# Hybrid decoder trunk: 43 elementwise instructions per MLP move from POOL to DVE

## The chip, the cores and the metric

The kernel runs on one core of one Trainium2 chip. The metric is the time of one execution on the device in microseconds (us), of which the median over several runs is given. The engines are called by their short names: PE is TensorE, PEld its weight loads, DVE VectorE, ACT ScalarE, POOL GpSimd, SP SyncE, whose queue (SPq) issues all of the kernel's DMAs.

## The reference, cut to what matters

The trunk takes 1024 tokens of width 1024, puts 16 meta tokens ahead of them, and runs two layers: a Mamba-2 mixer and an MLP, then a latent-attention mixer and an MLP. What the change touches is the beginning of each MLP:

```
def rms_norm(x, gain):
    y = xf * lax.rsqrt(jnp.mean(xf * xf, axis=-1, keepdims=True) + EPS)
    return (y * gain)
def sqrelu_mlp(h, w_up, w_down):
    return jnp.square(jax.nn.relu(h @ w_up)) @ w_down
...
h = h + sqrelu_mlp(rms_norm(h, ln_mlp[i]), mlp_w_up[i], mlp_w_down[i])
```

`w_up` is 1024 x 4096, `w_down` 4096 x 1024, all in float32.

## The kernel before

**Precision.** Each float32 operand is split into a hi part in the matmul's format (`fp32r`), made by an ACT cast, and a lo part, the source minus the hi part, made by a `tensor_tensor` on DVE or POOL. Each product is three matmuls: hi x hi, hi x lo, lo x hi (`mm_k`, lines 604 to 606 of the profile).

**Strassen's scheme.** Both matrix products of an MLP are done with Strassen's seven products in place of eight. Tokens are cut into two halves (520 each in MLP 0, 512 in MLP 1), the width of 1024 into two halves, and the 4096 hidden columns into 16 units of 256, each in two halves of 128. A unit has the products P1 to P7. P1 and P2 take the plain inputs; P6, P7, P5 and P4 take sums and differences of the input's quarters (`x_sums`), and of the unit's weight quarters (`block`). P3 takes another plain quarter.

**The order at the beginning.** The ones matmuls that give the normalisation are late on purpose in the program: products are made from the inputs times gain, and `hidden` multiplies by the reciprocal root mean square (`rb`) once it is known. First come P1 and P2 of eight units, 16 products (`pre`); their weights are loaded in pairs of units (`prep0`, line 794). Between them `x_sums(k)` makes the four summed inputs, a quarter of each at a time, and `rstd(0)` the normalisation of half 0, from the sum of squares that `sum_squares(0)` added up. Then P6, P7, P5 and P4 of unit 0 run together in four PSUM tiles (`first`), which are all the PSUM tiles there are in this phase. `sum_squares(1)`, the input of P3 and `rstd(1)` follow in the program, and then the items of units 0 to 15 one after another, each weight prepared three items ahead (`prep`).

**The weights' lo parts.** `w_item` (line 598 is its lo part, 596 its hi part on ACT) counts the weights (`lo_n`) and gives every odd one to POOL and every even one to DVE, unless the caller asks for DVE with `on_v`. The down projection always does.

**Buffers.** `whl` holds five split weights, `raw` two raw weight tiles of 1 MB, `pu` five partial products, `c11` two; `t1`, `t2`, `ta`, `tb` of `x_sums` have one buffer each. The loads of raw weights (lines 794 and 645) wait until the tile's last readers, the casts and lo parts, are done. All DMAs stand in SP's queue, in order.

**Order on each engine.** The program is written in the order above, and the order in which each engine runs its instructions is made when the kernel is built: a scheduler plays the program through with a cost model, takes the ready instruction that comes first in the program, and places the waits. On the chip each engine then runs its own list in that order.

**PSUM.** A product is evacuated by ACT (P1, line 714) or by DVE (`add`, line 710). `hidden` is line 681 (DVE) and 682 (ACT), with the DMA of line 684. The output projection ahead of MLP 0 and MLP 1 is evacuated by DVE into `h` (line 466).

Of the kernel before, what the change touches and what calls it, by code (L numbers as in the profile page):

```python
# [9 lines left out]
F32 = mybir.dt.float32  # L10
# [4 lines left out]
ALU = mybir.AluOpType  # L15
# [4 lines left out]
P = 128  # L20
# [26 lines left out]
def trunk(ctx: ExitStack, tc, x, meta, ln_mix, ln_mlp, w_in, conv_w, conv_b, dt_bias, a_log, d_skip,  # L47
# [3 lines left out]
    V, S, G, PE = nc.vector, nc.scalar, nc.gpsimd, nc.tensor  # L51
# [501 lines left out]
    HK = KD // 2  # L553
# [4 lines left out]
    def mlp(layer, tok, w, close_h):  # L558
# [22 lines left out]
        def raw_tile():  # L581
            return rawp.tile([P, 4 * n], F32, name="raw")
# [9 lines left out]
        def w_item(src, on_v=False):  # L592

            k, m = src.shape[1:]
            wt = whl.tile([P, 2, 512], F32R, name="whl")[:, :, :k * m].rearrange("p a (k m) -> p a k m", k=k)
            S.copy(wt[:, 0], src)  # L596
            lo_n[0] += 1
            (G if lo_n[0] % 2 and not on_v else V).tensor_tensor(wt[:, 1], src, wt[:, 0].bitcast(F32), ALU.subtract)  # L598
            return wt
# [22 lines left out]
        rb = misc.tile([P, 2, n], F32, name="rb")  # L622
# [9 lines left out]
        def pu():  # L632
            return misc.tile([P, n], F32, name="pu", bufs=5)

        class Unit:
# [33 lines left out]
            def prep(self, p):  # L669
                if p == "P6" and self.u < NPRE:  # L670
                    self.p1 = pu()
                    nc.sync.dma_start(self.p1, p1_d[self.u])
                self.W[p] = w_item(self.block(p))

            def hidden(self, half, i, name):

# [77 lines left out]

        def x_split(xt, k, src):
            S.copy(xt[:, k, 0, :], src)  # L756
            G.tensor_tensor(xt[:, k, 1, :], src, xt[:, k, 0, :].bitcast(F32), ALU.subtract)

        def sum_squares(half, new):
            for k in range(KD):  # L760
                src = h[:, k, hslice[half]]
                if k == 0:
                    S.activation(rb[:, half, :], src, AF.Square)
                else:
                    sq = new()
                    S.activation(sq, src, AF.Square)
                    G.tensor_tensor(rb[:, half, :], rb[:, half, :], sq, ALU.add)

        def rstd(half, new):

# [16 lines left out]
        units = [Unit(u) for u in range(NPRE)]  # L787
        pair = [None]

        def prep0(u, j):  # L790
            if j == 0:
                if u % 2 == 0:
                    pair[0] = raw_tile()[:, :KD * 2 * P].rearrange("p (i k m) -> p i k m", i=2, k=KD)
                nc.sync.dma_start(pair[0][:, u % 2], w_up[layer, :, u * 256:u * 256 + P].rearrange("(k p) m -> p k m", p=P))
            units[u].W["P%d" % (j + 1)] = w_item(pair[0][:, u % 2, j * HK:(j + 1) * HK, :])

        tmp_stack = ExitStack()
        tp = tmp_stack.enter_context(tc.tile_pool(reuse_waits="tile", name="utmp", bufs=1))
# [1 line left out]
        for a in pre[:4]:  # L800
            prep0(*a)
        for p, j in (("P1", 0), ("P2", 1)):
            for k in range(HK):
                x_plain(X[p], k, j, 0)
        sum_squares(0, pu)
        for half in range(2):
            nc.sync.dma_start(hsp[:, :, half, :], h[:, :, hslice[half]])

        def x_sums(k):
            g1, g2 = gcol_(k), gcol_(HK + k)  # L810
            h11, h12 = [h[:, k, s_] for s_ in hslice]
            h21, h22 = [h[:, HK + k, s_] for s_ in hslice]

            def tmp(name):
                return tp.tile([P, n], F32, name=name)

            b11, t1, t2 = tmp("ta"), tmp("t1"), tmp("t2")
            S.activation(b11, h11, AF.Copy, scale=g1)
            V.scalar_tensor_tensor(t1, h12, g1, b11, ALU.mult, ALU.subtract)
            V.scalar_tensor_tensor(t2, h22, g2, t1, ALU.mult, ALU.subtract)  # L820
            x_split(X["P6"], k, t2)
            b12 = tmp("ta")
            S.activation(b12, h12, AF.Copy, scale=g1)
            V.scalar_tensor_tensor(b12, h22, g2, b12, ALU.mult, ALU.subtract)
            x_split(X["P7"], k, b12)
            x_split(X["P5"], k, t1)
            b21 = tmp("tb")
            S.activation(b21, h21, AF.Copy, scale=g2)
            V.tensor_tensor(b21, t2, b21, ALU.subtract)
            x_split(X["P4"], k, b21)  # L830

        for i, (u, j) in enumerate(pre):
            if i + 4 < len(pre):
                prep0(*pre[i + 4])
            units[u].run("P%d" % (j + 1))
            if i == 1:
                rstd(0, pu)
            if i % 4 == 3:
                x_sums(i // 4)
# [3 lines left out]
        for k in range(HK):  # L843
            for p in ORDER[2:6]:
                mm_k(first[p], units[0].W[p], X[p], k, k == 0, k == HK - 1)
        sum_squares(1, lambda: tp.tile([P, n], F32, name="sq", bufs=2))
        tmp_stack.close()
        X["P3"] = up.enter_context(tc.tile_pool(reuse_waits="tile", name="ux3", bufs=1)).tile([P, HK, 2, n], F32R, name="xP3")
# [196 lines left out]
        for j, g in enumerate(prods):  # L1045
            f, c, p = g
# [67 lines left out]
    with ExitStack() as st:  # L1114
# [5 lines left out]
        sq = [sm.tile([P, T], F32, name=f"asq{i}") for i in range(2)]  # L1120
# [430 lines left out]
```

## Time and profile before

| | |
|---|---|
| median of 3 runs | 3000.17 us (2999.78 to 3005.01) |
| profiled execution | 3008.28 us |
| its span, first to last instruction | 3006.6 us |
| mean granted TensorE clock | 0.983 |
| PE busy | 2882.3 us, 96% of the span |
| DVE busy | 2231.1 us, 74% |
| ACT busy | 1283.4 us, 43% |
| POOL busy | 1114.1 us, 37% |

The span is one execution seen by the hardware profiler. An engine's busy time counts its instructions' own times, and waits inside an instruction once it has begun are in it. PE's matmuls are pipelined, so a listed matmul can be longer than the step to the next one. MLP 0 begins at about 960 us of the span (its first matmul at 982), MLP 1 at about 2336 us (first matmul at 2353).

### The profile page before, as it was taken

Reading aid. Unit: us, or ns where it says so; the run is one execution under the profiler, and the core shown is the slowest. Engines: PE = TensorE matmul, PEld = TensorE weight load, DVE = VectorE, ACT = ScalarE, POOL = GpSimd, SP = SyncE. Lnnn points to the kernel's source line nnn. Section 1 sums busy time; section 2 is a strip of 40 time slices with the busy share of each in tenths; the row PEclk is TensorE's granted clock in tenths of the full one; section 3 lists DMA queues with packets and bytes.
Section 4 is the critical chain, followed back from the end, with each engine's and each line's share of the span. In section 5 each row is a group of like instructions: output and inputs, shape, how many; then the busy total and the mean of one; then the engine's idle time right before and its main releaser. Section 6 shows DMA issues by size and latency. Waiting matters only on the chain. (4 is left out here: it accounts for less than half of the span.)

```text
span 3006.6 us, 48412 instructions
## 1 busy us (share of the span) xinstructions
PE 2882.3 (96%) x18221; PEld 2579.1 (86%) x18221; DVE 2231.1 (74%) x3904; ACT 1283.4 (43%) x2539; POOL 1114.1 (37%) x996
## 2 busy tenths in 40 slices
PE   7999999999899899999999889899999999999999
PEld 7999999999799899999999777677777777888887
DVE  6678877778856898875685477778774898876664
ACT  4334333334432633343443446456552643343442
POOL 2345444444764722210021454554554732210010
PEclk9999999999999999999999989899999999999999
DMA  3233333334633455479883101001132455479753
GB/s 110 63 70 78 63 73 72 73 70 105 170 111 97 163 179 198 154 264 359 306 285 106 44 23 26 20 27 33 30 120 87 155 175 203 161 280 342 265 182 104
DMA packets 326660, 409.32 MB, mean 136 GB/s; under 512 B 31341, under 2 KB 199234, under 8 KB 323354
## 3 DMA queue, kind: packets, MB, share of 16 engines
q1 hardware_dynamic: 326426, 406.24, 42.9%
q8 instruction: 143, 2.34, 0.3%
q14 instruction: 91, 0.75, 0.1%
HBM read 300.23 MB, written 105.88 MB: 135 GB/s over the span
## 5 line engine op out<-in xcount | busy, mean ns | idle before, releaser
L604 PE MATMUL mps<-hhl,whl 128*128 128x260 f32 (+1 forms) x1472 | 440.5, 300 | 8.5 <-DVE c L710 4.2
L606 PE MATMUL mps<-hhl,whl 128*128 128x260 f32 (+1 forms) x1472 | 436.6, 297 | 8.0 <-DVE whl L598 4.3
L605 PE MATMUL mps<-hhl,whl 128*128 128x260 f32 (+1 forms) x1472 | 437.7, 298 | 0.1
L98 PE MATMUL psm<-hn,whl 128*128 128x346 f32 (+4 forms) x1176 | 388.9, 331 | 6.0 <-DVE zs L269 4.4
L99 PE MATMUL psm<-hn,whl 128*128 128x346 f32 (+4 forms) x1176 | 386.5, 329 | 0.3 <-DVE hn L221 0.3
L100 PE MATMUL psm<-hn,whl 128*128 128x346 f32 (+4 forms) x1176 | 382.5, 326 | 1.1 <-POOL whl L93 1.1
L604 PEld LDWEIGHTS mps<-hhl,whl 128*128 128x128 f32 x1472 | 278.0, 189 | 19.1 <-issue 4.8
L606 PEld LDWEIGHTS mps<-hhl,whl 128*128 128x128 f32 x1472 | 279.0, 190 | 17.8 <-DVE whl L598 5.4
L605 PEld LDWEIGHTS mps<-hhl,whl 128*128 128x128 f32 x1472 | 278.2, 189 | 8.5 <-issue 0.5
L598 DVE TENSOR_TENSOR whl<-draw,whl 128x512 fp32r<-128x512 f32 x208 | 150.4, 735 | 172.5 <-ACT whl L596 172.4
L93 POOL TENSOR_TENSOR whl<-wraw,whl 128x1024 fp32r<-128x1024 f32 (+3 forms) x95 | 226.4, 2384 | 139.9 <-ACT whl L90 134.6
L596 ACT CAST whl<-draw 128x512 fp32r<-128x512 f32 x208 | 128.7, 622 | 324.8 <-PE mps L606 169.8
L604 PE MATMUL mps<-xP,whl 128*128 128x260 f32 (+1 forms) x768 | 246.5, 321 | 11.1 <-ACT xP L756 3.4
L606 PE MATMUL mps<-xP,whl 128*128 128x260 f32 (+1 forms) x768 | 245.9, 321 | 5.4 <-DVE whl L598 5.4
L605 PE MATMUL mps<-xP,whl 128*128 128x260 f32 (+1 forms) x768 | 246.1, 320 | 0.0
L98 PEld LDWEIGHTS psm<-hn,whl 128*128 128x128 f32 (+1 forms) x1176 | 220.9, 188 | 13.8 <-DVE zs L269 4.7
L100 PEld LDWEIGHTS psm<-hn,whl 128*128 128x128 f32 (+1 forms) x1176 | 220.6, 188 | 6.2 <-issue 3.3
L998 POOL TENSOR_TENSOR mP<-mP,mP 128x520 f32<-128x520 f32 (+1 forms) x28 | 43.3, 1568 | 492.5 <-DVE mP L995 432.6
L99 PEld LDWEIGHTS psm<-hn,whl 128*128 128x128 f32 (+1 forms) x1176 | 221.1, 188 | 4.8 <-issue 1.7
L598 POOL TENSOR_TENSOR whl<-raw,whl 128x512 fp32r<-128x512 f32 x64 | 95.4, 1494 | 217.8 <-ACT whl L596 96.5
L612 PE MATMUL mps<-whl,hhl 128*128 128x512 f32 x448 | 173.8, 389 | 0.3 <-DVE whl L598 0.3
L613 PE MATMUL mps<-whl,hhl 128*128 128x512 f32 x448 | 174.0, 389 | 0.0
(386 smaller groups left out, 7972.4 us busy)
## 6 DMA issues: line engine op xcount, KB each, us to landing
draw<-in_mlp_w_down_dram SPq DMA_DIRECT2D x52, 1024.0 KB
raw<-in_mlp_w_up_dram SPq DMA_DIRECT2D x32, 1024.0 KB
raw<-hid SPq DMA_DIRECT2D x28, 1040.0 KB
raw<-hid SPq DMA_DIRECT2D x28, 1024.0 KB
hid<-stg SPq DMA_DIRECT2D x96, 260.0 KB
wraw<-in_ssd_w_in_dram SPq DMA_DIRECT2D x48, 512.0 KB
hid<-stg SPq DMA_DIRECT2D x96, 256.0 KB
acsb<-acs_d SPq DMA_DIRECT2D x64, 256.0 KB
```

The lines of the kernel that those rows point to most:

```text
L93: eng_lo.tensor_tensor(lo, src, hi.bitcast(F32), ALU.subtract)
L98: PE.matmul(ps, whi, xhi, start=i == 0, stop=False)
L99: PE.matmul(ps, whi, xlo, start=False, stop=False)
L100: PE.matmul(ps, wlo, xhi, start=False, stop=i == n - 1)
L596: S.copy(wt[:, 0], src)
L598: (G if lo_n[0] % 2 and not on_v else V).tensor_tensor(wt[:, 1], src, wt[:, 0].bitcast(F32), ALU.subtract)
L604: PE.matmul(ps[:, i, :], wt[:, 0, k, :], xt[:, k, 0, xs_], start=first, stop=False)
L605: PE.matmul(ps[:, i, :], wt[:, 0, k, :], xt[:, k, 1, xs_], start=False, stop=False)
L606: PE.matmul(ps[:, i, :], wt[:, 1, k, :], xt[:, k, 0, xs_], start=False, stop=last)
L612: PE.matmul(ps[:, 0, :], xt[:, k, 0, qs], wt[:, 1, 0, :], start=False, stop=False)
L613: PE.matmul(ps[:, 0, :], xt[:, k, 1, qs], wt[:, 0, 0, :], start=False, stop=last)
L998: G.tensor_tensor(out_, out_, a, ALU.add)
```

## The change

Four edits in `mlp`, which runs twice. `x_split` and `sum_squares` call DVE (`V`) in place of POOL (`G`) for the lo part and for the addition. `prep0` asks `w_item` for DVE for all its 16 weights (P1 and P2 of eight units), and `prep` does so for units 0 and 1 (ten weights: P6, P7, P5, P4 and P3 of each). The counter `lo_n` still counts each weight, so the later weights keep their engines. Per MLP these are 2 x 7 additions, 16 lo parts of inputs and 13 lo parts of weights, since the other 13 of the 26 were on DVE before.

```
@@ -670 (Unit.prep)
-                self.W[p] = w_item(self.block(p))
+                self.W[p] = w_item(self.block(p), self.u < 2)
@@ -754 (x_split)
             S.copy(xt[:, k, 0, :], src)
-            G.tensor_tensor(xt[:, k, 1, :], src, xt[:, k, 0, :].bitcast(F32), ALU.subtract)
+            V.tensor_tensor(xt[:, k, 1, :], src, xt[:, k, 0, :].bitcast(F32), ALU.subtract)
@@ -764 (sum_squares)
                     S.activation(sq, src, AF.Square)
-                    G.tensor_tensor(rb[:, half, :], rb[:, half, :], sq, ALU.add)
+                    V.tensor_tensor(rb[:, half, :], rb[:, half, :], sq, ALU.add)
@@ -792 (prep0)
-            units[u].W["P%d" % (j + 1)] = w_item(pair[0][:, u % 2, j * HK:(j + 1) * HK, :])
+            units[u].W["P%d" % (j + 1)] = w_item(pair[0][:, u % 2, j * HK:(j + 1) * HK, :], True)
```

## Rows read from the trace of the kernel before

**Rows 1.** The page's first part: busy time, share of the span and instructions of each engine.

```profile
PE 2882.3 (96%) x18221; PEld 2579.1 (86%) x18221; DVE 2231.1 (74%) x3904; ACT 1283.4 (43%) x2539; POOL 1114.1 (37%) x996
```

**Rows 2.** The windows view of both beginnings; each engine's busy time and instruction count, granted clock.

```profile
982.00:1053.20 71.20, 60.03 (x468) 58.79 (x468) 62.27 (x59) 45.51 (x78) 54.02 (x33) 0.95 0.52 172
2353.00:2421.50 68.50, 59.22 (x232) 46.19 (x233) 60.91 (x60) 44.90 (x78) 53.19 (x33) 0.90 0.54 177
```

**Rows 3.** PE's timeline, its longest gaps: start, length, engine, line, [idle before <- releaser].

```profile
1011.58 0.39 PE L604 MATMUL mps<-hhl,whl 128*128 128x260 f32 x1 [1.94 <-DVE c L710]
...
1043.02 0.58 PE L604 MATMUL mps<-xP,whl 128*128 128x260 f32 x1 [2.89 <-ACT pu L714]
...
2391.04 0.50 PE L606 MATMUL mps<-hhl,whl 128*128 128x512 f32 x1 [2.25 <-POOL whl L598]
...
2410.88 0.80 PE L606 MATMUL mps<-xP,whl 128*128 128x512 f32 x1 [3.19 <-DVE whl L598]
```

**Rows 4.** PE's timeline where nothing holds it back: first and last of a run.

```profile
1047.68 0.28 PE L604 MATMUL mps<-xP,whl 128*128 128x260 f32 x1
...
1052.23 0.29 PE L606 MATMUL mps<-xP,whl 128*128 128x260 f32 x1
...
2418.11 0.40 PE L605 MATMUL mps<-hhl,whl 128*128 128x512 f32 x1
...
2421.97 0.39 PE L604 MATMUL mps<-xP,whl 128*128 128x512 f32 x1
```

**Rows 5.** DVE's and then POOL's timeline where both work.

```profile
1021.30 1.80 DVE L829 TENSOR_TENSOR tb<-t,tb 128x520 f32<-128x520 f32 x1
1023.03 1.77 DVE L656 TENSOR_TENSOR s<-raw 128x512 f32<-128x512 f32 x1
1024.73 0.68 DVE L710 TENSOR_TENSOR c<-pu,mps 128x520 f32<-128x520 f32 x1
...
1022.51 1.74 POOL L757 TENSOR_TENSOR hhl<-t,hhl 128x520 fp32r<-128x520 f32 x1
1024.22 1.71 POOL L598 TENSOR_TENSOR whl<-raw,whl 128x512 fp32r<-128x512 f32 x1
```

**Rows 6.** DVE's timeline where POOL is idle.

```profile
1004.23 0.75 DVE L819 SCALAR_TENSOR_TENSOR t<-h,prm,ta 128x520 f32<-128x520 f32 x1
1004.90 1.31 DVE L681 SCALAR_TENSOR_TENSOR c<-c,rb 128x520 f32<-128x520 f32 x2
...
2429.98 0.68 DVE L598 TENSOR_TENSOR whl<-s,whl 128x512 fp32r<-128x512 f32 x1
2430.58 0.68 DVE L775 TENSOR_SCALAR stg<-mps 128x512 f32<-128x512 f32 x1
```

**Rows 7.** The windows view of the sums of squares (line 767) ahead of the first beginning: POOL's busy time.

```profile
960.00:974.00 14.00, 10.98 (x7) 1.00 0.18 66
```

**Rows 8.** DVE's timeline at the end of the output projection ahead of MLP 0.

```profile
966.82 1.13 DVE L753 SCALAR_TENSOR_TENSOR hhl<-h,prm,hhl 128x520 fp32r<-128x520 f32 x1
967.87 0.75 DVE L466 TENSOR_TENSOR h<-h,psm 128x260 f32<-128x260 f32 x2
...
980.34 0.43 DVE L466 TENSOR_TENSOR h<-h,psm 128x260 f32<-128x260 f32 x1 [0.30 <-PE psm L100]
```

**Rows 9.** The waits view of the first beginning, then of the second: who waited for whom, us, times.

```profile
POOL whl L598 <- ACT whl L596: 7.2, 2, 6.9
POOL xP L757 <- ACT xP L756: 7.1, 2, 4.1
...
POOL xP L757 <- ACT xP L756: 6.1, 5, 2.6
...
POOL whl L598 <- ACT whl L596: 4.8, 3, 1.9
```

**Rows 10.** The DMA queue's (SPq) and DVE's timeline: a load and its first reader.

```profile
2385.27 0.38 SPq L645 DMA_DIRECT2D raw<-in_mlp_w_up_dram  x1
...
2392.03 1.21 DVE L656 TENSOR_TENSOR s<-raw 128x512 f32<-128x512 f32 x1 [0.49 <-DMA raw<-in_mlp_w_up_dram]
```

## The prediction

> **What bounds the kernel now.** I read the page's first part first: TensorE (PE) is busy for 96% of the span, DVE as the next engine for 74% [rows 1]. So a change on DVE and POOL can pay only where PE stands still or runs slowly, and only up to that loss. I next asked for PE's timeline around both places where the changed lines run, the beginnings of the two MLPs, and found a row of gaps there, of which the four shown last 1.9 to 3.2 us [rows 3]. Their releasers are of three kinds: a PSUM evacuation (line 710 on DVE, 714 on ACT) and a weight's lo part (line 598), on POOL or on DVE. The gap at 1043.02 stands with ACT's copy, which itself was queued behind work that waited for DVE.
>
> The windows view then sizes the loss. The first beginning is taken from the first MLP matmul to the first sum product (982 to 1053.2), the second likewise (2353 to 2421.5) [rows 2]. Where nothing holds PE back, 39 matmuls of 260 columns start in a row with 38 steps between 1047.68 and 1052.23, 0.1197 us each, and 17 steps of 512 columns take 3.86 us, 0.2271 us each [rows 4]. PE's own need is thus 468 x 0.1197 = 56.0 us of the 71.2, and 232 x 0.2271 = 52.7 us of the 68.5 [rows 2, 4]. What is lost is 15.2 and 15.8 us, 31.0 in all. Part of it is the clock: the mean granted clock is 0.95 and 0.90 in these windows [rows 2], since it falls to the lower level, 1.2 GHz, behind some of the gaps: the matmuls at 1043.02 and 2410.88 took 0.58 and 0.80 us, those behind two shorter gaps 0.39 and 0.50 [rows 3]. That loss goes if the gaps go.
>
> In both windows DVE is the fullest engine beside PE: 62.27 and 60.91 us, for only 59 and 60 instructions, more than 1 us each [rows 2]. The reason is in its timeline. Where POOL works too, a DVE instruction with two SBUF inputs takes 1.77 to 1.80 us and starts 1.7 us after the one before, POOL's own take 1.7 us and follow at that same step, and the two alternate; DVE's line 710, with one input in PSUM, takes 0.68 us in the middle of it [rows 5]. Where POOL is idle, the same kind of DVE instruction takes 0.68 us and the next starts after 0.60 us, and one with a scalar pointer after 0.67 us [rows 6]. So here a POOL instruction costs DVE about 1.1 us (1.7 less 0.60), more than the 0.60 us of doing that work itself.
>
> **The change, part by part.** *What moves.* Per MLP it is 7 adds per half of the tokens, 16 lo parts of input sums, and the half of 26 weight lo parts that POOL had: 14 + 16 + 13 = 43 instructions, of which POOL runs 33 inside each window [rows 2]. The seven adds of half 0 run ahead of it, with 10.98 us of POOL [rows 7]; the other lo parts lie at its edges.
>
> *DVE's load in the windows.* Of the 59 present instructions 16 (lines 753, 819, 820, 824, four each) are of the kind with a scalar pointer: 16 x 0.67 + 43 x 0.605 = 36.7 us without POOL beside them. The 33 added make 20.0 us. Together 56.7, against 62.27 now: DVE gains 5.6 us while it does more. In the second, 16 x 0.66 + 44 x 0.60 + 33 x 0.60 = 56.8 against 60.91: 4.1 us. (0.605 and 0.66 are the same steps at 520 and 512 columns, estimated from [rows 6].)
>
> *What the end gains.* From below: if DVE's queue sets the end and idles as long as now (8.9 and 7.6 us, window less busy time), the gain is 5.6 + 4.1 = 9.7 us. From above: if PE runs at its own pace throughout, 31.0 us. Both ends are close to one another in kind, since DVE's 56.7 us would just fit beside PE's 56.0. For the upper end speaks that some of DVE's work is not needed in time: the seven adds of half 1 (4.2 us), four of line 753 (2.7 us) and the sums of unit 1's weights feed only later products, and now they stand behind everything else. Against it speaks that two engines at full load in order never fit without gaps. I take the middle, 20.4 us.
>
> *The stretch before.* The adds of half 0 come to DVE while it evacuates the output projection (line 466). They add 7 x 0.60 = 4.2 us and take POOL's brake off line 753, which now takes a step of 1.05 us (966.82 to 967.87) in place of 0.67 [rows 8], 7 x 0.38 = 2.7 us: 1.5 us more per MLP. At most this delays PE by 3.0 us in sum, since PSUM buffers free later. At the least it costs nothing: the adds are needed only by the ones matmuls after unit 0, and later DVE idles 0.30 us before each line 466 [rows 8]. I take 1.5 us.
>
> *Queues.* POOL issues no DMA. SP's loads of later weights wait for lo parts, because those release the raw buffers; the lo parts come earlier, so the loads do too. A load of 1 MB was issued at 2385.27 and its first reader waited only 0.49 us for it at 2392.03 [rows 10], so a load takes 6.8 us and is not what holds this stage. On ACT nothing is added. Behind each moved lo part on DVE now stand the evacuations that give PE its PSUM buffer; that is the price of a misplaced one, 0.60 us plus whatever that lo part waits for on ACT.
>
> *Sum.* 20.4 less 1.5 is 18.9, say 19 us. The profiled execution took 3008.28 us (span 3006.6), 8.1 above the median of the runs; its windows go into the difference alone: 3000.2 less 19 is 2981 us.
>
> *A rule against it.* DVE is busy for 87% and 89% of the windows [rows 2], and POOL for 76% and 78%. The Trainium skill (Perfetto Trace Analysis, Optimizing Scalar/DVE Operations) says that work may be worth moving from a saturated DVE to GpSimd, which is the reverse of this change; in the same place it warns that the two share an SBUF read port, so that it might not help. By the rule without the warning this change would be slower, by the first rival's sum; the trace bears out the warning [rows 5, 6].
>
> **The rivals.** *DVE's present busy time is all its own.* Then the added work comes on top: 62.27 + 20.0 + 8.9 = 91.2 us in place of 71.2, and 20 us again in the second window, with 8.4 us of adds before them: +48, 3048 us. That is the case the skill's rule would make. Against it: the same line 598 at 0.68 us and the same line 656 at 1.77 [rows 5, 6]. Chance 0.03.
>
> *Waits for ACT move into DVE's queue* (the slower side). Each moved lo part needs ACT's cast of the same tile, just made. On POOL such waits were free: 7.2 + 7.1 us in the first window, 6.1 + 4.8 in the second, 25.2 in all [rows 9]. On DVE they stop evacuations. It decides at 9.7 us more of DVE idle, where the lower bound is used up. With all of them, 25.2 - 9.7 + 3.0 = +18.5: 3019 us. For it: ACT's casts in turn wait for DVE's sums, a round trip in the middle of every input sum. Against it: on DVE other ready instructions lie between, and POOL waited mostly because it had nothing else. Chance 0.09.
>
> *The same with about half of them*: 12.6 - 9.7 + 1.5 = +4.4, 3005 us, nothing that can be measured; or the gain is there and later stages take it back. Chance 0.14.
>
> *PE at its own pace in both windows, adds in DVE's gaps*: -31, 2969 us. Chance 0.05.
>
> **How the numbers follow.** The forecast has the other 0.69, and its own range is 2971 to 2993: the bounds 9.7 - 3.0 = 6.7 and 31.0 - 1.5 = 29.5 us below 3000.2. About 0.2% (6 us) is what a measurement of this kernel can tell from no change; the runs lie 5 us apart. Faster by more: 0.69 + 0.05 = 0.74; within: 0.14; slower: 0.03 + 0.09 = 0.12. The range reaches from 2970, almost at PE's own pace, to 3001, which takes in the nearer half of the cases without a change; left out are the slower ones (0.12), the other half (0.07) and some 0.01 below.
>
> **What would show it.** In the profile after, DVE's two-input instructions in both windows should take 0.68 to 0.76 us throughout, POOL should be nearly idle there, DVE's instruction count should rise by 33 per window while its busy time falls to about 57 us, and the first sum product should be evacuated about 10 us earlier after the first MLP matmul in each. PE's gaps of 2 to 3 us should mostly be gone and the clock at 1.00. It is wrong if DVE keeps its 1.8 us instructions with POOL idle, if DVE's waits for ACT grow past 5 us a window, or if the windows shrink and the span doesn't.

## The result and the profile after

The changed kernel takes 2973.2 us in the median of four runs (2966.9 to 2984.1), against 3002.1 for the kernel before in four (2999.8 to 3005.0). The ratio is 0.9896, with a 95% interval of 0.9875 to 0.9916: 28.9 us less. Measured a second time beside the kernel before, the changed kernel was 22.9 us faster (run e9 below). The profiled execution took 2973.4 us, its span is 2971.7.

The page's first part, which answers to [rows 1]:

```profile
PE 2871.9 (97%) x18221; PEld 2571.5 (87%) x18221; DVE 2225.1 (75%) x3990; ACT 1284.7 (43%) x2539; POOL 980.8 (33%) x910
```

POOL has 86 instructions and 133 us less, DVE 86 instructions more and 6 us less. That is the change in one line: 86 instructions were added to DVE and its busy time fell.

The windows view of the two beginnings, which answers to [rows 2]. Each window runs from the first MLP matmul to the evacuation of the first sum product; the columns are the window, its length, busy time (x instructions) of PE, PEld, DVE, ACT and POOL, the granted clock, the DMA share and GB/s:

```profile
977.20:1034.54 57.34, 57.30 (x475) 57.21 (x476) 54.85 (x90) 44.89 (x78) 0.00 (x0) 1.00 0.65 209
2332.99:2388.78 55.79, 55.31 (x242) 45.14 (x241) 54.91 (x91) 43.55 (x75) 0.00 (x0) 1.00 0.63 208
```

The same two windows in the kernel before, from its own first matmul to its own evacuation; the second began 1 us ahead of the 2353 that the prediction took:

```profile
982.35:1053.27 70.92, 60.10 (x468) 58.83 (x469) 61.92 (x58) 45.16 (x78) 54.02 (x33) 0.95 0.53 173
2351.98:2421.49 69.51, 59.89 (x235) 46.46 (x234) 61.92 (x61) 45.71 (x79) 53.31 (x33) 0.90 0.53 174
```

The first has shrunk from 70.9 to 57.3 us, the second from 69.5 to 55.8. POOL runs nothing in either. DVE runs 90 and 91 instructions in 54.9 us each, 0.609 and 0.603 us per instruction, and the granted clock is 1.00, its upper level of 2.4 GHz, in place of 0.95 and 0.90. PE's own need is now 475 x 0.1197 = 56.9 and 242 x 0.2271 = 55.0 us [rows 4]: it runs at its own pace but for 0.5 and 0.8 us. DVE is busy for 7.1 us less in the first window and 7.0 in the second than before, and idle for 6.5 and 6.7 us less.

DVE's timeline in a stretch like that of [rows 5], the same lines 829 and 656:

```profile
1012.86 0.70 DVE L829 TENSOR_TENSOR tb<-t,tb 128x520 f32<-128x520 f32 x1
1013.47 0.70 DVE L757 TENSOR_TENSOR hhl<-t,hhl 128x520 fp32r<-128x520 f32 x1
1014.08 0.69 DVE L656 TENSOR_TENSOR s<-s,raw 128x512 f32<-128x512 f32 x1
1014.68 0.70 DVE L710 TENSOR_TENSOR c<-pu,mps 128x520 f32<-128x520 f32 x1
```

Both took 1.8 us before and take 0.70 and 0.69 now, and the next one starts 0.61 and 0.60 us after them.

Not all of DVE's shorter busy time is the missing brake. Four instructions of line 753 stood inside each window before, the first of them at 1046.85 in MLP 0; in the new order they stand behind its end:

```profile
1046.85 0.75 DVE L753 SCALAR_TENSOR_TENSOR xP<-h,prm,xP 128x520 fp32r<-128x520 f32 x1
```

```profile
1034.54 0.70 DVE L710 TENSOR_TENSOR pu<-pu,mps 128x520 f32<-128x520 f32 x1 [1.43 <-PE mps L606]
1035.15 0.75 DVE L753 SCALAR_TENSOR_TENSOR xP<-h,prm,xP 128x520 fp32r<-128x520 f32 x1
```

At a step of 0.67 us they are 2.7 us per window that moved and weren't saved. Of the other side of the prediction's account, the end of the output projection [rows 8], here is DVE's timeline, and then the view of the projection's matmuls ahead of MLP 0 with their first and last start:

```profile
963.16 0.75 DVE L753 SCALAR_TENSOR_TENSOR hhl<-h,prm,hhl 128x520 fp32r<-128x520 f32 x1
963.83 0.42 DVE L466 TENSOR_TENSOR h<-h,psm 128x260 f32<-128x260 f32 x1
964.16 0.69 DVE L767 TENSOR_TENSOR rb<-rb,pu 128x520 f32<-128x520 f32 x1
964.78 0.42 DVE L466 TENSOR_TENSOR h<-h,psm 128x260 f32<-128x260 f32 x1
```

```profile
L100 PE MATMUL psm<-oact,whl x400: 277/318/511, 753.4 to 976.4; 128*128 128x348 f32 x57, 128*128 128x346 f32 x55, 128*128 128x260 f32 x22
```

The adds of line 767 now stand between the evacuations; line 753 starts 0.67 us ahead of the next instruction, not 1.05. From first to last matmul the projection takes 223.0 us, against 221.6 before (759.9 to 981.5). Of PE's gaps [rows 3] these remain, the first behind the window, the second at the very start of the other, the third in the later units, where POOL still makes half of the weights' lo parts:

```profile
1042.20 0.39 PE L604 MATMUL mps<-hhl,whl 128*128 128x260 f32 x1 [1.78 <-DVE pu L710]
...
2334.53 0.50 PE L606 MATMUL mps<-hhl,whl 128*128 128x512 f32 x1 [0.47 <-DVE whl L598]
...
2480.53 0.50 PE L606 MATMUL mps<-xP,whl 128*128 128x512 f32 x1 [1.26 <-POOL whl L598]
```

**Where the 34.9 us between the two spans went.** Shrunk windows 13.6 + 13.7 = 27.3; behind the second window 2.2; the projection ahead of MLP 0 cost 1.4. The rest, some 6.8 us, lies outside of what was changed: the Mamba mixer's first products (line 100), which the change doesn't touch, end at 743.1 us in place of 749.6. How far such stretches vary is seen in the changed kernel's second run: its windows sum up to 113.1 us again, but from the end of the first to the start of the second it took 1305.9 us, in place of 1298.5 here, and its median was 2980.5 us. Times of two kernels therefore differ by several us for reasons that don't concern the change, and where that matters the text below goes by the sum of the two windows, taken in each profile in the same way. It is 140.4 us before and 113.1 after.

### The profile page after: what moved, and what is told of

It reads as the page before. It is cut to its first block, busy times and chain, and to the rows that moved or that the text cites. A ratio compares the mean times of both kernels' runs of the same rounds, so it can differ in the third digit from the quotient of the medians.

```text
span 2971.7 us, 48357 instructions
## 1 busy us (share of the span) xinstructions
PE 2871.9 (97%) x18221; PEld 2571.5 (87%) x18221; DVE 2225.1 (75%) x3990; ACT 1284.7 (43%) x2539; POOL 980.8 (33%) x910
## 5 line engine op out<-in xcount | busy, mean ns | idle before, releaser
L598 POOL TENSOR_TENSOR whl<-s,whl 128x512 fp32r<-128x512 f32 x42 | 64.5, 1539 | 343.8 <-ACT whl L596 291.9
```

## The experiments

Two theories were set against each other. The *brake*: a POOL instruction that reads SBUF holds up DVE's two-input instructions, so that it costs DVE more than doing the work itself. The *latency*: DVE makes a lo part in 0.69 us where POOL needs 1.3 to 1.75, so what waits for it gets it sooner. A third, that the build's new order on each engine brought the gain, is tested beside them.

**The change in parts.** Three kernels move one part each, a fourth moves all lo parts and leaves all additions on POOL.

```
e1_inputs_only:     x_split alone:        G.tensor_tensor -> V.tensor_tensor
e2_weights_only:    w_item alone:         on_v=True in prep0, self.u < 2 in prep
e3_squares1_only:   sum_squares, half 1:  (V if half else G).tensor_tensor
e8_squares_on_pool: e1 and e2 together, sum_squares on G
```

> Only the 16 lo parts of input sums per MLP go to DVE. Brake theory (each POOL instruction with SBUF inputs costs DVE about 1.1 us, whatever it computes, against 0.60 us on DVE itself): 16 of the 33 instructions per window, so about half of the 26.3 us that the two windows shrank by, 10 to 15 us faster than before, some 2988 us, and two-input DVE instructions beside POOL's remaining ones still at 1.7 to 1.8 us. Latency theory (what pays is that the lo part which PE or ACT waits for is made in 0.69 us in place of 1.3 to 1.75): no PE gap of before was released by one of these lo parts, so 0 to 4 us.

> Only the 13 weight lo parts per MLP go to DVE. Brake theory: 10 of 33 per window, 6 to 10 us faster than before, some 2994 us. Latency theory: these are the lo parts that PE waited for (3.8 us of its gaps in the second window, and the weight loads behind them), so this part alone brings most of the gain, 15 us or more.

> Only the 7 additions of half 1 per MLP go to DVE; no product waits for them before the second normalisation. Brake theory: 7 of 33 per window, 4 to 8 us faster than before, some 2996 us. Latency theory: nobody waits for them, so they bring nothing or cost their 4 us of DVE per MLP: 3002 to 3008 us.

> The changed kernel with all 14 additions of squares per MLP on POOL as before: only the lo parts are on DVE. Brake theory: 7 instructions of POOL in each window cost DVE about 0.95 us each in place of 0.60, 2 to 3 us per window, and the stretch before it gains 1.4 us in MLP 0: 1 to 5 us slower than the changed kernel, 2974 to 2978 us, though the run with only these additions moved showed no gain at all. Latency theory: no product waits for them, 2970 to 2973 us.

The medians were 2983.6, 3001.9 and 3006.0 us against 3001.7 for the kernel before beside them, ratios 0.9940 (0.9918 to 0.9963), 0.9991 (0.9978 to 1.0005) and 1.0007 (0.9996 to 1.0018); the fourth 2987.3 against 3005.3, 0.9941 (0.9922 to 0.9960). The windows views in this order:

```profile
977.40:1039.43 62.03, 58.21 (x470) 56.88 (x471) 60.82 (x74) 45.96 (x79) 31.12 (x17) 1.00 0.59 191
2335.44:2398.22 62.78, 56.49 (x242) 44.51 (x241) 61.64 (x76) 45.94 (x79) 32.27 (x17) 1.00 0.56 186
```

```profile
976.50:1045.62 69.12, 60.11 (x468) 58.75 (x469) 64.30 (x69) 45.27 (x79) 37.86 (x23) 0.95 0.54 177
2337.16:2404.93 67.77, 59.00 (x235) 45.28 (x234) 64.02 (x72) 45.16 (x78) 37.49 (x23) 0.95 0.51 168
```

```profile
981.10:1053.71 72.61, 62.33 (x468) 60.11 (x469) 64.95 (x65) 45.43 (x78) 42.09 (x26) 0.95 0.53 169
2354.33:2422.37 68.04, 60.57 (x235) 46.49 (x234) 61.83 (x68) 45.47 (x78) 41.18 (x26) 0.92 0.55 178
```

```profile
976.60:1035.56 58.96, 58.57 (x482) 58.04 (x483) 58.89 (x86) 45.48 (x79) 11.07 (x7) 1.00 0.64 207
2332.26:2393.40 61.14, 59.33 (x254) 47.06 (x253) 60.53 (x88) 46.48 (x81) 11.89 (x7) 1.00 0.59 192
```

The build orders the instructions anew in each kernel, so a different number of matmuls stands ahead of a window's end. PE's own need in the table is that number times its step, 0.1197 and 0.2271 us [rows 4]; what remains of the window is lost. All are sums of both windows, in us.

| kernel | POOL instructions in each window | windows | PE's own need | lost |
|---|---|---|---|---|
| before | 33 | 140.4 | 109.4 | 31.0 |
| squares of half 1 moved (e3) | 26 | 140.7 | 109.4 | 31.3 |
| weights moved (e2) | 23 | 136.9 | 109.4 | 27.5 |
| inputs moved (e1) | 17 | 124.8 | 111.2 | 13.6 |
| inputs and weights moved (e8) | 7 | 120.1 | 115.4 | 4.7 |
| all moved, the changed kernel | 0 | 113.1 | 111.8 | 1.3 |

Moving the inputs alone saved 15.6 us of the windows, the weights alone 3.5, the squares alone nothing, the first two together 20.3. The squares brought 7.0 more once the rest was gone, but only 3.4 of them are lost time; for the others fewer matmuls stand ahead of the end, and line 753 stood inside the windows in e8 and not in the changed kernel.

The first part has the size that the brake theory expected, and is not the 0 to 4 us of the latency theory. But in that run DVE's busy time fell by only 1.1 and 0.3 us; what fell was its idle time, from 9.0 and 7.6 to 1.2 and 1.1 us. The second part fell short of what the brake theory expected, and of what the latency theory expected by far more. The third is a miss for the brake theory as it was put, a fixed price per POOL instruction, and it is what the latency theory expected. The fourth is a miss for both: 2987.3 us, where 2974 to 2978 and 2970 to 2973 were expected.

The DVE column says why a fixed price fails. With 0.609 us for each DVE instruction, as in the changed kernel, the rest of DVE's busy time in a window is what POOL costs it: in the first window 61.92 - 58 x 0.609 = 26.6 us for POOL's 33 instructions in the kernel before, 0.81 each; 25.4 for 26 in the third run, 0.98; 22.3 for 23 in the second, 0.97; 15.8 for 17 in the first, 0.93; 6.5 for 7 in the fourth, 0.93. In the second window the same sums give 0.75 in the kernel before, and 0.79, 0.88, 0.90 and 0.99. Counted in DVE's timelines, the 33 instructions stretched 28 of its two-input instructions beyond 0.9 us in either window; 26 stretched 25 and 23, 23 stretched 22 and 20, 17 stretched 17, 7 stretched 6. So POOL's many instructions in the kernel before hit fewer than one of DVE's each, and to take some away removes in part those that hit none: moving seven additions took 1.2 and 4.4 us of brake away and put 7 x 0.609 = 4.3 us of work on DVE in each window. Which ones miss, and why, no run shows. In the fourth run the time rose by more than the windows account for, 14 us against 7, as far as kernels measured at different times can be compared; its profile is that of its fastest run, 2979.0 of 2979.0 to 2994.0, so what the slower ones lost was not seen.

**POOL work that nobody waits for.** Three kernels are the changed kernel with POOL instructions added whose results are never used, at each of the 16 input sums and at each of the 7 additions of half 1, in both MLPs. The order of all instructions on PE, DVE, ACT and SP, as the traces list them, is exactly that of the changed kernel.

```
+ scr = tp.tile([P, n], F32, name="scr")
  # in x_split; likewise in sum_squares if half, where e4 adds and e11 copies its own source
e4_pool_reads:       + G.tensor_tensor(scr, h[:, k, hslice[0]], h[:, k, hslice[1]], ALU.subtract)
e11_pool_one_input:  + G.tensor_copy(scr, h[:, k, hslice[0]])
e5_pool_memsets:     + for _ in range(3): G.memset(scr, 0.0)
```

> The changed kernel with 23 more POOL instructions per MLP that nobody waits for: one subtraction of two SBUF tiles at each input sum, one addition at each square of half 1, their results never used. Brake theory: each holds up DVE by about 0.9 us, 55 + 23 x 0.9 = 76 us of DVE per window in place of 55, so windows of 70 to 76 us in place of 57 and 56, and 26 to 38 us slower than the changed kernel: 2999 to 3011 us, about the time of the kernel before. Latency theory, and the theory that the build's new order brought the gain: nothing waits for these results, so 2973 us.

> The same places as the run before, but each additional POOL instruction is three memsets of the same tile, which read nothing in SBUF. If the brake comes from what POOL reads, DVE stays at 0.69 us and the time at 2973 us. If any POOL work brakes DVE, then 1.8 us instructions on DVE again and 2990 us or more.

> The changed kernel with 23 more POOL instructions per MLP that nobody waits for, each a copy with one SBUF input. If POOL's reading from SBUF is what brakes DVE, one input is enough: DVE instructions at 1.3 to 1.8 us again, windows of 65 us or more, 2990 us or more. If it takes two inputs on both sides, 2973 us.

The medians: 3020.9 us with two inputs (ratio to the kernel before 1.0051, 1.0031 to 1.0071), 2983.5 with one (0.9941, 0.9922 to 0.9960; the changed kernel beside it 2980.5, with an interval that overlaps), 2975.1 with none (0.9899, 0.9880 to 0.9918). Two inputs: the windows view, then DVE's and POOL's timeline.

```profile
985.50:1063.04 77.54, 63.44 (x482) 62.00 (x483) 77.50 (x89) 45.23 (x77) 36.81 (x23) 0.93 0.46 152
2361.05:2438.70 77.65, 62.27 (x245) 47.58 (x244) 77.53 (x91) 45.23 (x76) 36.68 (x23) 0.92 0.44 149
```

```profile
1000.49 1.82 DVE L828 SCALAR_TENSOR_TENSOR ta<-h,prm,ta 128x520 f32<-128x520 f32 x1
1002.23 1.82 DVE L768 TENSOR_TENSOR rb<-rb,sq 128x520 f32<-128x520 f32 x1
...
994.96 10.28 POOL L758 TENSOR_TENSOR scr<-h 128x520 f32<-128x520 f32 x6
```

One input, the same views:

```profile
979.40:1041.79 62.39, 59.19 (x482) 58.32 (x483) 62.35 (x90) 44.89 (x77) 22.01 (x23) 1.00 0.57 189
2333.55:2396.44 62.89, 58.79 (x247) 46.60 (x245) 62.89 (x92) 44.84 (x76) 21.68 (x23) 0.97 0.56 184
```

```profile
994.83 1.11 DVE L757 TENSOR_TENSOR xP<-tb,xP 128x520 fp32r<-128x520 f32 x1
995.86 1.10 DVE L598 TENSOR_TENSOR whl<-raw,whl 128x512 fp32r<-128x512 f32 x1
...
978.97 16.41 POOL L758 COPY scr<-h 128x520 f32<-128x520 f32 x16 [23.14 <-PE psm L100]
```

No input:

```profile
978.90:1036.19 57.29, 57.29 (x475) 57.17 (x476) 55.09 (x89) 45.01 (x78) 36.57 (x69) 1.00 0.65 210
2333.22:2389.22 56.00, 55.52 (x243) 45.31 (x242) 55.12 (x92) 43.96 (x75) 36.16 (x69) 1.00 0.64 207
```

```profile
989.29 0.69 DVE L757 TENSOR_TENSOR xP<-tb,xP 128x520 fp32r<-128x520 f32 x1
989.90 0.69 DVE L598 TENSOR_TENSOR whl<-raw,whl 128x512 fp32r<-128x512 f32 x1
...
996.77 0.81 DVE L785 TENSOR_SCALAR pu<-pu 128x520 f32<-128x520 f32 x1
...
984.92 10.60 POOL L759 MEMSET scr<- 128x520 f32 x18
```

The first of these decides between the theories. Nothing waits for these 23 instructions and no engine's order changed, yet the windows grew from 113.1 to 155.2 us, past the 140.4 of the kernel before, and the changed kernel became slower than that; the time lies above the 2999 to 3011 us that the brake theory gave. So the new order alone doesn't make the kernel fast; that it adds nothing, as with line 753, isn't shown. DVE is busy for all of both windows; its instructions beside POOL's take 1.8 us and step at 1.74, and 77.50 - 89 x 0.609 = 23.3 us are lost on 23 instructions of POOL, 1.01 us each. A copy with one input takes POOL 0.97 us, and DVE's two-input instructions then step at 1.03: 0.33 us lost for each, windows of 125.3 us. That lies between the two outcomes that were expected, 65 us or more for each window and no effect at all, and the medians alone don't tell it from the changed kernel. Three memsets in its place kept POOL busy for 36.6 us, about the same as the 23 reading instructions, and DVE's two-input instructions stayed at 0.69: 113.3 us. So it is POOL's reading of SBUF that brakes DVE, and a stretched DVE instruction steps as POOL's own do beside it: 1.74 us against 10.28 / 6 = 1.71, and 1.03 against 16.41 / 16 = 1.03. The Trainium skill (SBUF — State Buffer, Who interferes with whom) says this of a DVE instruction with two SBUF inputs: it contends with a GpSimd instruction that reads SBUF, not with one that only writes it. The three runs agree, with 1.8, 1.1 and 0.69 us.

**Additions of half 0, and the remaining weights.**

```
e6_half0_on_pool:        after, sum_squares: (V if half else G).tensor_tensor
e7_all_weights_dve:      after, prep: w_item(self.block(p), True)
e12_all_weights_again:   the same kernel as e7
e10_weights_half0:       e7 and e6 together
e9_after_again:          the changed kernel
```

> The changed kernel, with the 7 additions of half 0 back on POOL, which run beside the end of the output projection. The prediction's term for that stretch: they cost 1.5 us per MLP at most on DVE, so 0 to 3 us faster than the changed kernel, some 2972 us, with the first MLP matmul 1.4 us sooner after the projection's first. If the price of the adds is instead hidden, no difference; if the brake on line 753 and on the first splits matters more than the adds, up to 4 us slower, 2977 us.

> The changed kernel with all weight lo parts of the up projection on DVE, those of units 2 to 15 too. Brake theory: about 56 POOL instructions per MLP cost DVE some 0.9 us each and would cost 0.60 there, so DVE's queue loses up to 17 us per MLP of work, but PE stands still there for only a few us in all: 2 to 8 us faster than the changed kernel, 2965 to 2971 us. If a full DVE sets the pace and the brake is of no account, 5 to 30 us slower, since 34 us of work per MLP come on top.

> The changed kernel once more, on the same chip as the next two, so that small differences can be read: 2970 to 2976 us by every theory.

> All weight lo parts of the up projection on DVE, once more beside the changed kernel. If the 4 us of the first comparison are real, 2 to 6 us faster than the changed kernel in this call; if not, within 2 us.

> The same with the additions of half 0 back on POOL. The projection ahead of MLP 0 took 221.6 us with them there and 223.0 with them on DVE, so 1 to 2 us faster than the run before it if the windows stay at 57 and 54 us, and the fastest of all; equal if the first window pays it back.

With half 0 on POOL the projection takes 221.6 us again (753.7 to 975.3), so the 1.4 us are those adds; the windows view:

```profile
976.20:1033.49 57.29, 57.29 (x475) 57.17 (x476) 54.72 (x90) 44.82 (x78) 0.00 (x0) 1.00 0.65 209
2329.37:2386.12 56.75, 56.74 (x247) 45.76 (x245) 55.83 (x92) 45.84 (x79) 0.00 (x0) 1.00 0.63 204
```

The windows sum up to 114.0, and the median of 2974.7 us (ratio 0.9906, 0.9889 to 0.9923) can't be told from the changed kernel's. The changed kernel run again took 2980.5 us beside 3003.4 for the kernel before (0.9924, 0.9907 to 0.9941), outside of the 2970 to 2976 that was expected by every theory. All weight lo parts on DVE gave 2969.2 us (0.9879, 0.9860 to 0.9897), and, beside that second run of the changed kernel, 2976.6 (0.9907, 0.9887 to 0.9926): 4 us faster than the changed kernel both times, though the first time they weren't measured beside one another, with intervals that overlap. With both edits it was 2968.3 us (0.9878, 0.9858 to 0.9899), 12 us below the changed kernel measured beside it and with an interval clear of its own; 1 to 2 us below the run with all weights was expected, and it is 8. Its windows don't show this (114.4 us); behind the second one its profile has 577.0 us where the changed kernel's has 583.0, and why isn't shown. It has the lowest median here; but the ratio of one and the same kernel moved by 0.003 between two measurements, and 0.9879 was reached without the additions on POOL, so how much of the 12 us it has everywhere isn't settled. The windows view of the same stretch in the later units, the changed kernel and then this one, shows what the last step does:

```profile
2400.00:2500.00 100.00, 97.69 (x428) 79.49 (x427) 97.48 (x140) 36.77 (x60) 33.76 (x18) 1.00 0.63 214
```

```profile
2400.00:2500.00 100.00, 100.00 (x442) 82.34 (x441) 96.02 (x160) 40.20 (x65) 0.00 (x0) 1.00 0.63 211
```

With POOL out of it DVE ran 20 instructions more in less busy time, and PE, which had stood still for 2.3 us, had none of it.

## Why the prediction was right

It had the direction, the mechanism and a range that holds the time; its size, 19 us against 28.9, was too small, and 2973.2 us lies near the end of its range, close to the 2969 of the rival with PE at its own pace. Point by point:

- *A POOL instruction costs DVE about 1.1 us, the work itself 0.60.* The second is 0.609. The first was too high for the kernel before: 0.81 and 0.75 on average, and 0.79 to 1.01 where POOL's two-input instructions are fewer. That it is not a fixed price, the prediction did not see; its sum didn't use it, since it counted DVE's load without POOL directly.
- *DVE's load 56.7 and 56.8 us.* It was 54.9 and 54.9, for 90 and 91 instructions in place of 92 and 93. The sum counted four of line 753 (2.7 us) that left each window, and missed others that came in.
- *The window's gain, the middle between 9.7 and 31.0: 20.4.* This is the term that was mis-sized. It was 27.3. The lower bound supposed that DVE would idle as long as before, 8.9 and 7.6 us; it idled 2.5 and 0.9 (57.34 - 54.85, 55.79 - 54.91). Of the time that PE lost, 70.9 - 56.0 = 14.9 and, with the window from 2351.98, 69.5 - 235 x 0.2271 = 16.1 us, it still loses 0.5 and 0.8. Nearly the upper bound was the case, and two engines at nearly full load did fit. Of its reasons for that end, the one of line 753 came true; the additions of half 1 don't stand behind everything else, they ran between 981.5 and 1000 us. What is left between 29.7 and 27.3 us is that PE now runs 7 matmuls more in each window, ahead of its end. The middle was a choice between two bounds with no reason of its own.
- *The stretch before, 1.5 us in all, 3.0 at most.* 1.4 us in MLP 0 and, by the projection's matmuls, 119.9 us before and 120.1 after, 0.2 in MLP 1: 1.6. That the halved bound came out is luck: one MLP paid nearly all of its 1.5 us, the other next to nothing.
- *A later gain of nothing.* Behind the second window the kernel is 2.2 us faster; no run was made for that alone.
- *The rule against it*, that a full DVE be relieved by POOL, would have given 3048 us. DVE was busy for 87% and 89% of the windows before and for 96% and 98% after; what counts is that POOL's help was charged to it.
- *The rival of waits for ACT.* POOL had waited 25.2 us for ACT's casts; DVE now waits 1.0 us for ACT in the first window and 0.9 in the second, as the prediction's argument against this rival had it.

DVE's own idle time fell too, and that is 13.2 of the 27.3 us. The longest wait of the first window shows one way, before and after:

```profile
997.37 1.31 DVE L778 TENSOR_TENSOR pu<-pu 128x520 f32<-128x520 f32 x1 [2.94 <-ACT pu L777]
```

```profile
990.19 0.70 DVE L778 TENSOR_TENSOR pu<-pu 128x520 f32<-128x520 f32 x1 [0.64 <-ACT pu L777]
```

DVE's line 775 starts the normalisation, ACT's lines 776 and 777 follow, each with a table load of 1.28 us ahead of it in both kernels, and DVE's line 778 needs what they make. Between lines 775 and 778 DVE had two instructions before and has eleven now, six of them of lines 757 and 767, which were POOL's: the added work fills DVE's wait. Of the other waits no run separated how much the brake made and how much the lateness of POOL's or ACT's results. What is shown is that POOL's reading alone, put back beside an unchanged order, costs more than the whole gain.

## What to carry to other kernels

Before POOL takes elementwise work off a full DVE, look at DVE's instructions beside it: if those with two SBUF inputs take 1.8 us where the same line takes 0.7 alone, POOL's help is charged to DVE, and here at 0.75 to 1.0 us against 0.61 for the work itself. The price is not the same for each instruction, so that moving one set may bring nothing (e3) and another more than half of the gain (e1): try the whole set before judging by a part. To see whether an engine's instructions hold up another, add some that nobody waits for; if the others' order stays and their durations grow, they are held up by it.

## What the runs showed of the hardware that was not expected

Memsets on POOL left DVE's two-input instructions at 0.69 us, yet one DVE instruction was slowed by them: the `tensor_scalar` with one SBUF input and an SBUF output (line 785 of that kernel, in the fence above) took 0.81 us and 0.63 in the other MLP, where the changed kernel's took 0.42. In the kernel before, beside POOL's two-input instructions, it took 0.93 and 1.52 (line 780). The memset that began while it ran took 0.70 and 0.69 us in the two MLPs, all others 0.53 or 0.54. So here a POOL instruction that reads nothing and this one DVE instruction slowed each other; two instances each are too few to say more, and no run shows what they share.
